# Loading the first pair's summed block beside the last convolution, in buffers of its own, in a hybrid Hyena and attention layer

## The chip, the cores and the metric

One core of a Trainium2 chip. The metric is the device time of one execution in microseconds (us). The kernel before was timed in three runs, and one execution was recorded by the hardware profiler. Five engines take part: TensorE (PE, with its weight loads PEld), VectorE (DVE), ScalarE (ACT), GpSimd (POOL) and SyncE (SP). [...]

## The reference

One layer works on 640 tokens (128 of a prompt, 512 latent tokens on a grid of 8 rows by 64 columns), 1024 channels and 16 heads of 64. All of it is float32.

```python
h = x * (1 + scale) + shift                      # scale, shift from the conditioning vector
z = h @ w_in                                     # 1024 x 10240: Hyena 3+1, q, k, v, gate, two mixing gates
v_h, x1, x0 = split(short_conv(hy))              # taps of three tokens
y_h = (fft_conv(v_h * x1, filter) + v_h * x1 * d) * x0
y_a = softmax(q k^T / 8 + bias, window + context) @ [v, ctx_v]   # prompt: all keys of the prompt
p_h = (y_h * silu(g_h)) @ w_bh
p_a = (y_a * silu(g_a)) @ w_ba
out = (sigmoid(m_h) * p_h + sigmoid(m_a) * p_a) @ w_out
x   = layer_norm(ALPHA * x + gate * out)
```

The outputs are the new x of both groups and the keys and values of the prompt.

## The kernel before

Float32 accuracy comes from three passes per product: each operand is split into a high part and a low part, and high x high, high x low and low x high are added up in PSUM. The 640 columns of tokens go through TensorE in two halves of 320. A weight tile of 1024 x 128 comes as `raw`; ACT copies its high part (`wh`), and the low part (`wl`) is made from the difference.

The first 360 us compute the modulation, the Hyena projections, the long convolution by quarters (its last part is `long_conv(3)` and `long_conv_back(3)`, with the stores of its gated result `yu` to `yu_d`), and values, queries, keys and two mixing gates of the first tiles. In this stretch a scheduler orders the instructions of each engine; `weave` lays `hand_over()` beside the last convolution. Instructions keep the order that the schedule gives them on each engine, and a DMA queue's engine stands still in front of an issue whose wait has not ended.

From about 360 us on the order is written out by hand (`manual_schedule`). First `first_gates()` makes two gate tiles (`gate_a`, the matmuls `mm` at L182) and the first weight blocks. Then follow 21 pairs. A pair is two tiles of `w_in`, multiplied with the tokens by a scheme of seven block products instead of eight (`pair_tile`): each product j of `ORDER = ("b11", "t2", "t3", "t1", "b21", "t4", "b22")` takes one weight block of 512 x 128 (here 128 x 512 on chip) and half of the columns, and is 12 matmuls of 320 columns. `t1` to `t4` are sums of token halves that were stored in `tok_d` before and come back by `load_sums` (names `t_00` to `t_11`: the first digit is the half of the rows, the second is high or low part). For a pair p the weight blocks are, in the order of products:

- `ra` left half, b11; loaded whole by `load_a` (512 KB);
- `s1`, the sum of s2 and a22, made by DVE in `sum1` (L1175), which after `sum6` (L1179) also serves as the last block;
- `s2` (in the trace `s<-wall`): a load of 256 KB, onto which POOL adds a second block of the weights with an accumulating DMA (L1167);
- `s3`: likewise, loaded by SP into half of `rb` and accumulated at L1168 (`rb_q` for the first pair);
- `ra` right half; `a22` (the other half of `rb`, or `rb_ql`).

For each block ACT makes the high part (`high`, L1185) and DVE the low part (`low`, L1193), `AHEAD = 4` blocks before TensorE uses it. TensorE's matmuls of the pairs are at L1232 (`sp` in PSUM; `t` or `hH`, `hL` the tokens). What a pair gives is used by `later` functions, run one or several half-blocks on (`tick`). `scratch()` copies second halves of the tokens inside `hH` and `hL`; it can start when the last matmul of the second gate tile has read them.

Between the half-blocks the loop calls `attend`: a visit is `tiled(i)` (scores of two blocks of a head at L947, PE; their reduction on DVE at L973, exponentials on ACT at L981, scaling on POOL at L1002 and L1004, and the products with the values of the blocks two visits before) or `turned(i)` (transposes of the probabilities at L1031, copied by ACT at L1026 as `pts`). Scores, transposes and products share the auxiliary PSUM banks. For the first head three visits are taken by a rule that begins after eight half-blocks; that gives half-blocks 9, 15 and 22 of 28.

In `hand_over` the mixing tiles `mx` (tanh at L870 on ACT) are stored to `mh_d` by SP's queue (L871). The first pair's blocks come from `first_blocks`: s2 takes a row of the pool `yhp` (tag "yh"), s3 and a22 the buffers "q" and "ql" of the slots of a later head.

## Time and profile before

| what | value |
|---|---|
| three runs | 904.39, 905.91, 906.86 us; median 905.91 |
| profiled execution | 904.75 us, its span 903.0 us |
| mean granted TensorE clock | 0.988 |
| PE busy | 872.3 us, 97% of the span, 6476 matmuls |
| DVE / ACT / POOL busy | 637.4 (71%) / 450.0 (50%) / 189.9 us (21%) |
| moved by DMA | 169.09 MB, mean 187 GB/s |

A row of the timeline gives the start, the duration, the engine, the line, the operation, out<-in, the shape and a count when rows are merged; in brackets stands how long the engine was idle before and what ended that. "x2" on a merged row means that its first instruction starts there and the duration covers both. For a DMA the duration on the issuing engine (SPq, POOLq) is the issue; the time to landing is listed on its own.

### The profile page before, as it was taken

How to read it: one execution, taken by the hardware profiler on the slowest of the kernel's cores; microseconds unless marked ns; L12 is line 12 of the kernel's file. 1: busy time of each engine (PE TensorE's matmuls, PEld its weight loads, DVE VectorE, ACT ScalarE, POOL GpSimd, SP SyncE). 2: the span in 40 equal slices, each digit the busy share in tenths (PEclk: the TensorE clock that was granted, in tenths of full speed). 3: DMA queues.
4: the chain of work that ended last, by engine and by line, in shares of the span. 5: the costliest groups of instructions: out<-in, count | busy, mean ns of one | idle time of the engine just before them, and what ended most of it. 6: DMA issues, size and time to landing. Idle time of an engine off the chain costs nothing. (4 is left out here: it accounts for less than half of the span.)

```text
span 903.0 us, 17145 instructions
## 1 busy us (share of the span) xinstructions
PE 872.3 (97%) x6476; PEld 841.3 (93%) x6476; DVE 637.4 (71%) x1215; ACT 450.0 (50%) x956; POOL 189.9 (21%) x216
## 2 busy tenths in 40 slices
PE   8999999999999999879999999999999999999995
PEld 7789999999899999779999999999999999999884
DVE  4896574984786557279777778777877677667566
ACT  4485545645554545156666665656566632233200
POOL 0020111210110110126354334433545200000000
PEclk9999999999999999889999999999999999999998
DMA  8976666876557685877686758576845586555332
GB/s 334 404 205 136 140 163 151 223 175 154 138 120 164 180 197 115 304 216 225 185 221 165 211 168 233 150 219 171 229 115 141 189 299 230 164 166 188 115 104 85
DMA packets 75247, 169.09 MB, mean 187 GB/s; under 512 B 11004, under 2 KB 28668, under 8 KB 75165
## 3 DMA queue, kind: packets, MB, share of 16 engines
q1 hardware_dynamic: 56492, 123.72, 41.5%
q0 software_dynamic: 13632, 39.33, 22.8%
q10 hardware_dynamic: 5040, 4.95, 1.6%
q8 instruction: 51, 0.84, 0.4%
q14 instruction: 32, 0.25, 0.1%
HBM read 143.32 MB, written 23.99 MB: 185 GB/s over the span
## 5 line engine op out<-in xcount | busy, mean ns | idle before, releaser
L1232 PE MATMUL sp<-t,wb 128*128 128x320 f32 x1008 | 161.1, 314 | 5.1 <-ACT wb L1185 5.1
L1232 PEld LDWEIGHTS sp<-t,wb 128*128 128x128 f32 x1008 | 152.3, 191 | 6.0 <-ACT wb L1185 5.4
L1232 PE MATMUL sp<-hH,wb 128*128 128x320 f32 x500 | 121.1, 313 | 0.0
L182 PE MATMUL mm<-hH,wh 128*128 128x320 f32 x336 | 84.1, 316 | 9.6 <-ACT mx L870 4.2
L1232 PEld LDWEIGHTS sp<-hH,wb 128*128 128x128 f32 x500 | 85.9, 188 | 2.8 <-issue 2.8
L182 PE MATMUL mm<-hL,wh 128*128 128x320 f32 x336 | 82.2, 313 | 0.4 <-DVE hL L329 0.4
L182 PE MATMUL mm<-hH,wl 128*128 128x320 f32 x336 | 81.5, 312 | 0.4 <-DVE wl L102 0.4
L1232 PE MATMUL sp<-hL,wb 128*128 128x320 f32 x250 | 77.3, 309 | 0.0
L162 POOL DMA_DIRECT2D wl<-wall x34 | 30.4, 893 | 220.7 <-ACT wl L161 201.8
L182 PEld LDWEIGHTS mm<-hH,wh 128*128 128x128 f32 x336 | 57.7, 190 | 12.0 <-ACT mx L870 4.4
L163 ACT ACTIVATE wh<-raw 128x1024 fp32r<-128x1024 f32 x34 | 36.2, 1064 | 63.0 <-PE mm L182 47.9
L1185 ACT ACTIVATE wb<-s 128x512 fp32r<-128x512 f32 x63 | 39.7, 631 | 42.8 <-PE sp L1232 19.4
L182 PEld LDWEIGHTS mm<-hL,wh 128*128 128x128 f32 x336 | 57.7, 190 | 1.5 <-DVE hL L329 1.2
L182 PEld LDWEIGHTS mm<-hH,wl 128*128 128x128 f32 x336 | 57.6, 190 | 1.3 <-DVE wl L102 0.9
L1193 DVE TENSOR_TENSOR wb<-s,wb 128x512 fp32r<-128x512 f32 x63 | 45.0, 716 | 18.8 <-ACT wb L1185 18.7
L1002 POOL TENSOR_SCALAR p<-p,sm 128x384 f32<-128x384 f32 x32 | 50.3, 1667 | 22.0 <-DVE sm L1000 15.8
L1002 POOL TENSOR_SCALAR edge<-edge,sm 128x320 f32<-128x320 f32 x32 | 41.7, 1405 | 52.1 <-DVE sm L1000 52.1
L1232 PEld LDWEIGHTS sp<-hL,wb 128*128 128x128 f32 x250 | 47.0, 188 | 0.0
L1509 PE MATMUL out<-woh,yhs 128*128 128x512 f32 (+1 forms) x176 | 45.7, 373 | 0.0
L1220 DVE TENSOR_TENSOR spare_hHp<-sp,yu 128x320 f32<-128x320 f32 x63 | 30.5, 483 | 16.8 <-PE sp L1232 11.5
L182 PE MATMUL mm<-yhs,wh 128*128 128x320 f32 x224 | 42.0, 309 | 0.0
L1509 PEld LDWEIGHTS out<-woh,yhs 128*128 128x128 f32 x176 | 32.0, 188 | 6.2
(415 smaller groups left out, 2251.7 us busy)
## 6 DMA issues: line engine op xcount, KB each, us to landing
raw<-wall SPq DMA_DIRECT2D x54, 512.0 KB, 3.9
wl<-wall POOLq DMA_DIRECT2D x34, 512.0 KB, 6.7
ra<-wall SPq DMA_DIRECT2D x21, 512.0 KB, 4.0
rb<-wall SPq DMA_DIRECT2D x40, 256.0 KB, 4.5
ada<-wada SPq DMA_DIRECT2D x16, 512.0 KB, 7.9
tm<-bias SPq DMA_DIRECT2D x16, 512.0 KB, 6.9
s<-wall SPq DMA_DIRECT2D x21, 256.0 KB, 4.7
s<-wall POOLq DMA_DIRECT2D x21, 256.0 KB, 4.6
```

What stands on the lines that cost most here:

```text
L162: nc.gpsimd.dma_start(wl, a["wall"][i], accum_op=ALU.add)
L163: nc.scalar.activation(wh, raw[:], AF.Copy)
L182: nc.tensor.matmul(ps[hf][:, :HALF], wt[k], x[:, hf * HALF : (hf + 1) * HALF], start=(i == 0 and k == 0), stop=(i == lead[2] and k == NK - ...
L1002: nc.gpsimd.tensor_scalar_mul(pv, pv, sm[:, 2, c : c + 1])
L1185: nc.scalar.activation(made[g][:, 0], sums_[g // 7][g % 7], AF.Copy)
L1193: nc.vector.tensor_tensor(made[g][:, 1], sums_[g // 7][g % 7], f(made[g][:, 0]), op=ALU.subtract)
L1220: nc.vector.tensor_tensor(c, dst, c if j == 3 else ps["u"], op=ALU.add)
L1232: nc.tensor.matmul(dst, wk, x(xi, k), start=j < 4 and k == 0 and i == 0, stop=k == 3 and i == 2, skip_group_check=True,)
L1509: ins = nc.tensor.matmul(dst, m[k][:, c0 : c0 + P], w[:, c : c + n], start=(first and k == 0), stop=(last and k == 5), skip_group_check=True,)
```

## The change

The change has five parts.

1. `first_blocks()` is called as soon as the slots exist, ahead of the values of the first head, instead of at the end of `hand_over`.
2. The sums get buffers of their own: `s2` one in `slots_q` for even pairs and one in `sp` for odd pairs, `s1` one in `sp`; before, they shared three buffers in `sp`. `ra` is taken up when it is needed (`block(g)`). In each pair the load of s2 now stands ahead of the two of rb. Of the buffers for the token sums, four are in `sp` and three in `tp` (before three and four).
3. The two stores of mixing tiles go out from ScalarE's queue.
4. The loads behind the hand-over are put in another order; those of t1, ra_1, t4 and the bias tiles (tm) follow `scratch()`.
5. The first head's three visits come after half-blocks 14, 20 and 27.

```diff
@@ hand_over
         out["slots_q"] = left.enter_context(tc.tile_pool(name="slots_q", bufs=1))
+        first_blocks()
         yield from chain(values(0), queries(0), keys(0))
...
         load_a(0)
-        first_blocks()
@@ mix_tile
-        nc.sync.dma_start(mh_d[n], th[:])
+        nc.scalar.dma_start(mh_d[n], th[:])
@@ attention_setup
-        homes[:] = [(sp, "tr", 3)] * 3 + [(tp, "tr", 4)] * 4 + [(yhp, "yh", NK + 1)]
+        homes[:] = [(sp, "tr", 4)] * 4 + [(tp, "tr", 3)] * 3 + [(yhp, "yh", NK + 1)]
@@ load_b, first_blocks, blocks
-        s2 = sp.tile([P, 512], F32, tag="s", bufs=3, name=f"s2_{p}")[:]
...
-        s2 = row(yhp, "yh", "s2_0")[:, :512]
...
+        s2 = (sp if p % 2 else out["slots_q"]).tile([P, 512], F32, tag="s", name=f"s2_{p}")[:]
+        load_to(s2, w0[:, :512])
         load_to(s3, w1[:, :512])
         load_to(a22, w1[:, 512:])
-        load_to(s2, w0[:, :512])
-        ra = raws.pop(("a", p))
-        sums_[p] = [ra[:, :512], None, s2, s3, ra[:, 512:], a22, None]
+        sums_[p] = [None, None, s2, s3, None, a22, None]
@@ sum1
-        s_[1] = s_[6] = sp.tile([P, 512], F32, tag="s", bufs=3, name=f"s1_{p}")[:]
+        s_[1] = s_[6] = sp.tile([P, 512], F32, tag="s1", name=f"s1_{p}")[:]
@@ after the hand-over
-    load_sums(1, SUMS[:2])
-    load_a(1)
+    load_sums(1, SUMS[:1])
     sums_of_second = load_b(1)
-    load_sums(1, SUMS[2:3])
-    biases[0] = [bias_tile(0)]
-    load_sums(0, SUMS[3:])
-    load_sums(1, SUMS[3:])
-    biases[0].append(bias_tile(1))
+    load_sums(1, SUMS[1:2])
...
         sums_of_second()
         scratch()
+        load_sums(1, SUMS[2:3])
+        load_a(1)
+        load_sums(0, SUMS[3:])
+        load_sums(1, SUMS[3:])
+        biases[0] = [bias_tile(h) for h in range(2)]
@@ the loop over heads
-                while taken * (n_main - late) < (done - late) * n_side:
+                while done in (14, 20, 27) if j == 0 else taken * n_main < done * n_side:
                     if next(side, StopIteration) is StopIteration:
                         break
                     taken += 1
+                    if j == 0:
+                        break
```

SP's queue around the hand-over, before. `t_10_4306` and `t_11_4308` are t2, 4310 and 4312 are t3, 4321 and 4323 are t1 (second half of the rows); `s_0` is the first pair's s2, `s_1` the second's. (In the changed kernel L1165, L1166 and L1234 are what L1167, L1168 and L1232 are before.)

```order
L63 DMA t_10_4306<-tok_d 128x640
L63 DMA t_11_4308<-tok_d 128x640
L871 DMA mh_d<-mx_4157 128x640
L63 DMA t_10_4310<-tok_d 128x640
L63 DMA t_11_4312<-tok_d 128x640
L63 DMA ra_4314<-wall 128x1024
L871 DMA mh_d<-mx_4218 128x640
L63 DMA rb_4316<-wall 128x512 x2
L63 DMA s_1_4317<-wall 128x512
L63 DMA s_0_4295<-wall 128x512
L63 DMA t_10_4321<-tok_d 128x640
L63 DMA t_11_4323<-tok_d 128x640
```

The same place after (t2, then s_1 and rb, t3 as 4315 and 4317, the scratch copies, t1 as 4450 and 4452):

```order
L63 DMA t_10_4306<-tok_d 128x640
L63 DMA t_11_4308<-tok_d 128x640
L63 DMA s_1_4311<-wall 128x512
L63 DMA rb_4310<-wall 128x512 x2
L63 DMA t_10_4315<-tok_d 128x640
L63 DMA t_11_4317<-tok_d 128x640
L63 DMA hH<-hHp 128x320 x2
L63 DMA hL<-hLp 128x320 x2
L63 DMA t_10_4450<-tok_d 128x640
L63 DMA t_11_4452<-tok_d 128x640
L63 DMA ra_4454<-wall 128x1024
```

The stores and the load of s_0 have left this stretch, and the loads of t1 and of `ra` stand behind the scratch copies.

POOL's queue, which issues the accumulating loads, from the last weight tiles of the scheduler's part on; before:

```order
L162 DMA wl_4054<-wall 128x1024
L1168 DMA rb_q<-wall 128x512
L162 DMA wl_4161<-wall 128x1024
L162 DMA wl_4222<-wall 128x1024
L162 DMA wl_4284<-wall 128x1024
L162 DMA wl_4289<-wall 128x1024
...
L1167 DMA s_1_4317<-wall 128x512
L1168 DMA rb_4316<-wall 128x512
L1167 DMA s_0_4295<-wall 128x512
```

and after:

```order
L162 DMA wl_4062<-wall 128x1024
L1165 DMA s_0_3755<-wall 128x512
L162 DMA wl_4169<-wall 128x1024
L1166 DMA rb_q<-wall 128x512
L162 DMA wl_4230<-wall 128x1024
L162 DMA wl_4292<-wall 128x1024
L162 DMA wl_4297<-wall 128x1024
...
L1165 DMA s_1_4311<-wall 128x512
L1166 DMA rb_4310<-wall 128x512
```

The accumulation onto s_0 moves from the end of the hand-over to the second row, and that of `rb_q` one place back.

TensorE's queue at the third visit, the transposes of the first head (`pt`), with what follows them; before:

```order
L1031 MATMUL pt_0_1_4801<-pack_380,p_0_1_4584 128x128 x3
L1031 MATMUL pt_1_1_4806<-pack_380,p_1_1_4585 128x128 x3
L1232 MATMUL sp_0_4674<-hH,wb_4687 128x320
L1232 MATMUL sp_0_4674<-hL,wb_4687 128x320
L1232 MATMUL sp_0_4674<-hH,wb_4687 128x320 x2
L1232 MATMUL sp_0_4674<-hL,wb_4687 128x320
L1232 MATMUL sp_0_4674<-hH,wb_4687 128x320 x2
```

and after, where the scores of the next head (`s_0_4891`) come two half-blocks later:

```order
L1031 MATMUL pt_1_1_4857<-pack_380,p_1_1_4646 128x128 x3
L1234 MATMUL sp_3_4752<-hH,wb_4724 128x320
L1234 MATMUL sp_3_4752<-hL,wb_4724 128x320
L1234 MATMUL sp_3_4752<-hH,wb_4724 128x320 x2
L1234 MATMUL sp_3_4752<-hL,wb_4724 128x320
L1234 MATMUL sp_3_4752<-hH,wb_4724 128x320
L1234 MATMUL sp_0_4876<-hH,wb_4764 128x320
L1234 MATMUL sp_0_4876<-hL,wb_4764 128x320
L1234 MATMUL sp_0_4876<-hH,wb_4764 128x320 x2
L1234 MATMUL sp_0_4876<-hL,wb_4764 128x320
L1234 MATMUL sp_0_4876<-hH,wb_4764 128x320
L947 MATMUL s_0_4891<-k_4565,q_4578 128x128
```

The transposes have moved to the end of the pair's visits, and only two half-blocks lie between them and the next scores; before, seven did.

More of the change, by code (lines that the diff above doesn't have):

```diff
@@ L1150, in load_b, with blocks @@
         rb = sp.tile([P, 1024], F32, tag="rb", bufs=2, name=f"rb{p}")
-        s2 = sp.tile([P, 512], F32, tag="s", bufs=3, name=f"s2_{p}")[:]
-        return blocks(p, s2, rb[:, :512], rb[:, 512:])
+        return blocks(p, rb[:, :512], rb[:, 512:])
     def first_blocks():
-        s2 = row(yhp, "yh", "s2_0")[:, :512]
-        blocks(0, s2, *(out["slots_q"].tile([P, NT], F32, tag=t, name=f"rb0_{t}")[:, :512] for t in ("q", "ql")))()
-    def blocks(p, s2, s3, a22):
+        blocks(0, *(out["slots_q"].tile([P, NT], F32, tag=t, name=f"rb0_{t}")[:, :512] for t in ("q", "ql")))()
+    def blocks(p, s3, a22):
         w0, w1 = (a["wall"][i] for i in pairs[p])
+        s2 = (sp if p % 2 else out["slots_q"]).tile([P, 512], F32, tag="s", name=f"s2_{p}")[:]
+        load_to(s2, w0[:, :512])
         load_to(s3, w1[:, :512])
         load_to(a22, w1[:, 512:])
-        load_to(s2, w0[:, :512])
-        ra = raws.pop(("a", p))
-        sums_[p] = [ra[:, :512], None, s2, s3, ra[:, 512:], a22, None]
+        sums_[p] = [None, None, s2, s3, None, a22, None]
         def summed():
@@ L1170, in blocks, with block @@
         return summed
+    def block(g):
+        p, j = divmod(g, 7)
+        return raws["a", p][:, 512 * (j // 4) : 512 * (j // 4) + 512] if j in (0, 4) else sums_[p][j]
     def sum1(p):
         s_ = sums_[p]
-        s_[1] = s_[6] = sp.tile([P, 512], F32, tag="s", bufs=3, name=f"s1_{p}")[:]
+        s_[1] = s_[6] = sp.tile([P, 512], F32, tag="s1", name=f"s1_{p}")[:]
         nc.vector.tensor_tensor(s_[1], s_[2], s_[5], op=ALU.add)
@@ L1178, in sum6 @@
         s_ = sums_[p]
-        nc.vector.tensor_tensor(s_[6], s_[4], s_[6], op=ALU.add)
+        nc.vector.tensor_tensor(s_[6], block(7 * p + 4), s_[6], op=ALU.add)
     def high(g):
@@ L1184, in high @@
             made[g] = wp.tile([P, 2, 512], F32R, tag=tag, bufs=2 if tag == "wh" else 3, name=f"wb{g}")
-            nc.scalar.activation(made[g][:, 0], sums_[g // 7][g % 7], AF.Copy)
+            nc.scalar.activation(made[g][:, 0], block(g), AF.Copy)
         elif (g - 7 * len(pairs)) % 2 == 0:
@@ L1192, in low @@
         if g < 7 * len(pairs):
-            nc.vector.tensor_tensor(made[g][:, 1], sums_[g // 7][g % 7], f(made[g][:, 0]), op=ALU.subtract)
+            nc.vector.tensor_tensor(made[g][:, 1], block(g), f(made[g][:, 0]), op=ALU.subtract)
         elif (g - 7 * len(pairs)) % 2:
@@ L1329, in yh_home @@
             return slot(0, ("q", "ql", "k", "kl")[i], f"yhs{i}", F32R)[:, :NT]
-        return row(yhp, "yh", f"yhs{i}", F32R)[:] if i < 13 else row(tp, "tr", f"yhs{i}", F32R, 4)[:]
+        return row(yhp, "yh", f"yhs{i}", F32R)[:] if i < 13 else row(tp, "tr", f"yhs{i}", F32R, 3)[:]
     yhH, yhL, yraw = [], [], {}
@@ L1374, in tile_hyena_natten_step @@
         scratch()
+        load_sums(1, SUMS[2:3])
[3 more added lines that the diff above has]
+        biases[0] = [bias_tile(h) for h in range(2)]
         for j in range(8):
-            late = 8 if j == 0 else 0
-            side, n_main, n_side = attend(j), N_PAIR * len(HEADS[j].split()), {0: 3, 7: N_ATT + 3}.get(j, N_ATT)
+            side, n_main, n_side = attend(j), N_PAIR * len(HEADS[j].split()), N_ATT if j < 7 else N_ATT + 3
             done = taken = 0
```

## The prediction

> **What bounds the kernel.** I read the page's head first, then the list of TensorE's waits, its timeline around the longest ones, and the window table for clock and transfers.

> ```profile
> span 903.0 us, 17145 instructions
> PE 872.3 (97%) x6476; PEld 841.3 (93%) x6476; DVE 637.4 (71%) x1215; ACT 450.0 (50%) x956; POOL 189.9 (21%) x216
> ...
> PEclk9999999999999999889999999999999999999998
> ```

> TensorE (PE) is busy 97% of the span, so time can only come from its few idle stretches and from slices below full clock. The two 8s inside the clock row are slices 17 and 18 of 22.6 us each (361 to 406 us), the place of the change. The list of TensorE's waits begins with the same place:

> ```profile
> PE sp L1232 <- ACT wb L1185: 5.1, 1, 5.1
> PE mm L182 <- ACT mx L870: 4.2, 1, 4.2
> ```

> No other single wait exceeds 1.8 us. The timeline of TensorE shows both, and what the 36 matmuls of three weight blocks take behind the second and at full clock:

> ```profile
> 365.53 0.96 PE L182 MATMUL mm<-hH,wh 128*128 128x320 f32 x2 [4.19 <-ACT mx L870]
> ...
> 381.62 0.31 PE L1232 MATMUL sp<-hH,wb 128*128 128x320 f32 x1
> ...
> 388.67 7.88 PE L1232 MATMUL sp<-t,wb 128*128 128x320 f32 x36 [5.13 <-ACT wb L1185]
> 396.38 0.31 PE L1232 MATMUL sp<-hH,wb 128*128 128x320 f32 x1
> ...
> 406.47 5.46 PE L1232 MATMUL sp<-t,wb 128*128 128x320 f32 x36
> ```

> Windows (the columns are PE, weight load, DVE, ACT, POOL busy with counts, granted clock, DMA share, GB/s):

> ```profile
> 365.50:370.00 4.50, 4.47 (x17) 4.43 (x18) 0.00 (x0) 1.07 (x3) 0.78 (x5) 0.53 0.95 302
> 370.00:381.60 11.60, 11.60 (x81) 11.60 (x80) 1.54 (x3) 1.28 (x3) 2.70 (x3) 1.00 1.03 376
> 383.40:388.60 5.20, 0.14 (x1) 0.00 (x0) 0.69 (x1) 0.61 (x2) 0.00 (x0) 0.82 0.79 196
> 388.60:396.40 7.80, 7.73 (x37) 7.51 (x38) 7.08 (x13) 4.33 (x10) 0.00 (x0) 0.68 0.67 214
> ```

> Each gap costs twice: the idle time, then about half clock (0.53, 0.68) until the clock is granted again. The second gap's cause, followed back through DVE, ACT, POOL and SP's queue:

> ```profile
> 387.26 0.69 DVE L1175 TENSOR_TENSOR s<-s,rb_ql 128x512 f32<-128x512 f32 x1 [10.56 <-DMA s<-wall]
> 387.99 1.15 ACT L1185 ACTIVATE wb<-s 128x512 fp32r<-128x512 f32 x2 [12.01 <-DVE s L1175]
> 376.53 0.90 POOL L1167 DMA_DIRECT2D s<-wall  x1 [10.25 <-DMA s<-wall]
> 365.83 0.32 SPq L871 DMA_DIRECT2D mh_d<-mx  x1
> 370.38 1.20 SPq L63 DMA_DIRECT2D s<-wall  x2
> ```

> SP loads s_0 as the second of the two rows at 370.38. POOL's accumulate onto it is the third of its run that starts at 376.53, and only when that lands can DVE make the sum (387.26), and ACT the weight block that TensorE waits for. The gap is a late load, not work.

> **The change, part by part.** *Early s_0.* After the change s_0's load stands directly ahead of rb_q's, and its accumulate one place ahead of rb_q's old one:

> ```profile
> 318.56 0.33 SPq L63 DMA_DIRECT2D rb_q<-wall  x1
> ...
> 325.79 0.90 POOL L1168 DMA_DIRECT2D rb_q<-wall  x1 [8.77 <-DMA raw<-wall]
> ```

> So s_0 is complete near 331 us, 45 us before use. What then sets the sum is the order on DVE and ACT, where it follows the first block:

> ```profile
> 374.69 0.77 ACT L499 ACTIVATE sg<-mm 128x320 f32<-128x320 f32 x2 [7.09 <-PE mm L182]
> 376.01 0.69 DVE L1193 TENSOR_TENSOR wb<-ra,wb 128x512 fp32r<-128x512 f32 x1
> ```

> Sum at 376.7, two blocks' high and low parts (0.6 to 0.7 each) done by 379.3; TensorE asks for them at 383.4. The margin is 4.1 us, so the wait of 5.13 goes: −5.13. Without it the clock has been at 1.00 since 370 and nothing lowers it, so the three blocks take 5.46, not 7.88: −2.42. [...] The rows have the loss itself, 2.42, and I go by them. The early stretch pays one more issue of 0.33 on SP and 0.9 on POOL, both waiting there anyway (8.77 idle): 0.

> *Stores of the mixing tiles on ScalarE's queue.* Two issues of about 0.33 under ACT's idle 7.09: 0. What is behind them on ACT is the second tanh, whose wait is this:

> ```profile
> 366.84 0.77 ACT L870 ACTIVATE mx<-mm 128x320 f32<-128x320 f32 x2 [1.04 <-DMA yu_d<-yu]
> yu_d<-yu POOLq DMA_DIRECT2D x4, 320.0 KB, 3.5
> ```

> It waits for one of POOL's stores; with SP's loads no longer held behind the tiles, more transfers compete with that. The tanh frees PSUM for the second gate tile, which TensorE does not begin before 373 (the first one's matmuls end near ACT's row at 374.69), so the store may land 6 us later than it did, beside a median of 3.5: 0. The first gap's wait (4.19) stays: its end is DVE's yu and ACT's tanh, and none of the change is ahead of them.

> *Loads after the hand-over.* s_1, rb_1 and t3 go out by about 369; then SP waits for the last reader of the scratch copies (hH, hL), and t1, ra_1, four t4 and the bias tiles tm follow:

> ```profile
> 376.30 1.60 SPq L63 DMA_DIRECT2D hH<-hHp  x2
> hH<-hHp SPq DMA_DIRECT2D x2, 160.0 KB, 10.8
> t<-tok_d SPq DMA_DIRECT2D x16, 320.0 KB, 6.0
> DMA to landing us min/median/max: 3.2/6.0/10.1
> tm<-bias SPq DMA_DIRECT2D x4, 512.0 KB, 5.3
> ```

> (The fourth row is for t in 300 to 400 us.) Now blocks follow each other every 1.76 us (381.62 to the end at 383.38), so t1's second half is asked for at 387.7 and t4's halves at 390.4 and 391.3. t1 is issued near 379.2 to 380.6: landing 385.6 with the median 6.0, and at worst 10.1 → 389.7, 2.0 late. In the built program each load on SP's queue also waits for the landing of the eighth load ahead of it: for t4_01, t4_10 and t4_11 those are scratch copies. These took 10.8 behind some 3 MB (two rb, two s, two t1, tm, three t4) that SP had issued just ahead. After the change what was issued earlier, some 3.2 MB from 359.6 on, is through by about 370 at 302 to 376 GB/s, so I take a copy at the quick end, 3.2 to 6: t4 issued by 383, there by 389. Cost 0; bounds 0 and 387.4 + 6.0 − 390.4 = 3.0. tm issued near 384 lands at 389 to 391, asked for at 395.5: 0.

> *Own buffers.* One s, one s1 and a lazily taken ra instead of shared tags; later pairs load s_2 first and then rb. TensorE's longest two waits both end before 389, and no wait of a weight block is listed after that, so later there is nothing to gain, and blocks made four ahead (7 us) cover a load shifted by one issue: 0.

> *Visits.* Scores of the first head move from half-block 9 to 14 (TensorE near 394), the next from 15 to 20, transposes from 22 to 27. Distances among these stay, but the next head's scores stand two half-blocks (1.8 us) behind the transposes, not seven. Rows of before:

> ```profile
> 397.36 0.33 PE L947 MATMUL s<-k,q 64*128 64x128 f32 x2
> 411.77 0.82 PE L1031 MATMUL pt<-pack,edge 128*128 128x128 f32 x6
> ...
> 412.29 0.87 ACT L1026 ACTIVATE pts<-pt 128x384 f32<-128x384 f32 x2 [0.94 <-PE pt L1031]
> 413.57 0.87 ACT L1026 ACTIVATE pts<-pt 128x384 f32<-128x384 f32 x2
> ...
> 408.20 1.18 POOL L1004 TENSOR_SCALAR pp<-pp,sm 128x128 f32<-128x128 f32 x2
> 403.00:411.70 8.70, 8.70 (x64) 8.32 (x63) 8.40 (x25) 7.10 (x22) 6.31 (x7) 1.00 0.47 100
> ```

> From the first scores to POOL's end is 12.0 us (397.36 to 409.38), to the transposes 14.4; 13 half-blocks keep that. The copies of the transposes end 2.7 us after these start (414.44 − 411.77), and the next scores, which take those PSUM banks, come after 3.1: margin 0.4. One weight copy of 0.64 ahead of them makes 0.2 late, two make 0.9. ACT was busy 7.10 of 8.70 there, so I take 0.5 between 0 and 0.9.

> Sum: 904.75 (the profiled execution, span 903.0 and 1.75 around it) − 5.13 − 2.42 + 0.5 = 897.7, a change of −7.05. The median of the three runs, 905.91, is 1.16 above the profiled one; from it the same change gives **898.9 us**. A measurement here tells about 0.3% (2.7 us) from no change.

> **Rivals.** *Late second-half loads* (t1 or t4 behind the scratch copies). For: the 10.8 us landing and the wait on the eighth load before; against: the queue ahead is empty by then. Price 2 to 3 us of idle, so 900.9 to 901.9. Whether that idle also lowers the clock no row decides: this one of 1.77 did not, while 4.19 and 5.13 did.

> ```profile
> 238.35 0.41 PE L182 MATMUL mm<-hH,wh 128*128 128x320 f32 x1 [1.77 <-ACT zs L484]
> 240.00:244.00 4.00, 4.00 (x29) 4.00 (x28) 4.00 (x10) 1.49 (x3) 0.56 (x1) 1.00 0.83 261
> ```

> If it does, 2.1 to 2.4 more: 904.3 at worst, inside "same". [...]

> *Moved visits stall TensorE like a gap*: the transposes or next scores wait 3.5 us or more (POOL's chain has 2.4 us to spare) and the clock falls: 898.9 + 3.5 + 2.4 = 904.8, no difference.

> *The change does not do it*: the sum still waits, for instance since DVE's queue holds it behind something of the hand-over: 905.9.

> *Slower*: visits now share pair 1 with the next head's. In 403 to 411.7 DVE is busy 8.40 of 8.70, and a visit's own DVE rows run from 398.43 to 401.2:

> ```profile
> 398.43 0.49 DVE L973 CUSTOM_DVE_ANT_0 edge<-s,tm 128x320 f32<-128x320 f32 x1 [1.35 <-PE s L947]
> ...
> 400.81 0.48 DVE L991 TENSOR_REDUCE sm<-s 128x1 f32<-128x128 f32 x2
> ```

> If those 2.8 us, with ACT's part (about 3) in turn, delay the weight blocks past their lead of 7 us (it decides once DVE's backlog exceeds that lead), TensorE waits in each of two pairs for 2.8 + 3: 11.6 − 0.5 more, 910. Against: backlog of about 3 us is less than half the lead.

> **Chances.** Forecast 0.67; late loads 0.17; stalling visits 0.06; no effect 0.05; slower 0.05. The forecast's own range is 897 to 900. For 8 in 10 the range needs the late loads as well, without most of the clock loss: 896.5 to 903.0, whose lower end is the full 7.55 with no stall (898.4) less the spread of the runs shown (1.5 below their median). Faster by over 0.3% (below 903.2): 0.67 + 0.16 = 0.83. Same: 0.01 of late loads, 0.06, 0.05: 0.12. Slower 0.05.

> **What the changed profile would show.** Right: no row of a weight block among TensorE's waits above 1 us, the 4.2 on the tanh still first; clock 1.00 from 370 to 400; three blocks in about 5.5 us from 383.4; DVE's sum near 377; POOL's accumulate onto s near 326; a span near 896. Wrong: a wait of t matmuls for a load (late loads), scores or transposes waiting for ACT or POOL above 1.5 us (visits), the sum still near 387 (no effect), or weight-block waits of 2 us and more after 400 (slower).

## The result and the profile after

The changed kernel takes 899.1 us (median of four runs, 897.27 to 900.61), the kernel before 905.97 (904.39 to 906.86). The ratio is 0.9925, with a 95% interval of 0.9902 to 0.9948: 4.7 to 8.9 us less. The forecast was 898.9, range 896.5 to 903.0. The profiled execution took 897.27 us, 7.48 less than the profiled one of before, at a mean clock of 0.993 instead of 0.988.

The head of the page, and the first three of TensorE's waits:

```profile
span 895.5 us, 17141 instructions
...
PEclk9999999999999999899999999999999999999998
```

```profile
PE mm L182 <- ACT mx L870: 4.2, 1, 4.2
PE mm L182 <- ACT hH L328: 2.9, 3, 1.3
PE mm L182 <- ACT zs L484: 2.4, 2, 1.8
```

One of the two 8s of the clock row is gone, and so is the wait of 5.1 us for a weight block; the wait for the tanh of the mixing tile is as long as it was. TensorE's timeline at the two places (L1177, L1187 and L1195 of the changed kernel are what L1175, L1185 and L1193 are before):

```profile
365.89 0.96 PE L182 MATMUL mm<-hH,wh 128*128 128x320 f32 x2 [4.22 <-ACT mx L870]
...
383.71 0.31 PE L1234 MATMUL sp<-hHp,wb 128*128 128x320 f32 x1
383.86 5.47 PE L1234 MATMUL sp<-t,wb 128*128 128x320 f32 x36
389.16 0.31 PE L1234 MATMUL sp<-hH,wb 128*128 128x320 f32 x1
```

The three blocks of t matmuls follow the first block without a gap and take 5.47 us instead of 7.88. The chain that had made them late, in the timelines of SP, POOL, DVE and ACT:

```profile
318.91 0.33 SPq L63 DMA_DIRECT2D s<-wall  x1
325.94 0.88 POOL L1165 DMA_DIRECT2D s<-wall  x1 [8.60 <-DMA new_v<-v]
377.03 0.69 DVE L1177 TENSOR_TENSOR s<-s,rb_ql 128x512 f32<-128x512 f32 x1
377.75 1.15 ACT L1187 ACTIVATE wb<-s 128x512 fp32r<-128x512 f32 x2 [1.36 <-DVE s L1177]
```

The load now goes out at 318.9 and the accumulate at 325.9; DVE makes the sum at 377.0 directly behind its preceding row, without waiting, and the first two weight blocks are ready four us ahead of use (VectorE's low parts of both end by 379.7, TensorE takes the first at 383.86). The loads that stood in doubt:

```profile
376.13 1.34 SPq L63 DMA_DIRECT2D hH<-hHp  x2
378.87 1.02 SPq L63 DMA_DIRECT2D t<-tok_d  x2
380.47 1.80 SPq L63 DMA_DIRECT2D t<-tok_d  x4
382.32 1.78 SPq L63 DMA_DIRECT2D tm<-bias  x2
DMA to landing us min/median/max: 2.0/2.1/2.1
```

(The last row is the landing of the two copies into hH, from SP's issues.) They took 2.1 us, not 10.8, so nothing behind them was held. The wait that did grow is the second tanh's, hidden as forecast:

```profile
369.81 0.77 ACT L870 ACTIVATE mx<-mm 128x320 f32<-128x320 f32 x2 [3.65 <-DMA yu_d<-yu]
```

It was 3.0 us later than before (366.84), and TensorE does not ask for its PSUM before 373.

### The profile page after: what moved, and what is told of

Read it like the earlier page. It is cut to its first block, busy times and chain, and to the rows that moved or that the text cites. A ratio compares the mean times of both kernels' runs of the same rounds, so it can differ in the third digit from the quotient of the medians.

```text
span 895.5 us, 17141 instructions
## 1 busy us (share of the span) xinstructions
PE 870.1 (97%) x6476; PEld 839.2 (94%) x6476; DVE 637.4 (71%) x1215; ACT 450.3 (50%) x956; POOL 190.2 (21%) x216
## 3 DMA queue, kind: packets, MB, share of 16 engines
q0 software_dynamic: 13632, 39.33, 22.6%
## 5 line engine op out<-in xcount | busy, mean ns | idle before, releaser
L1234 PE MATMUL sp<-t,wb 128*128 128x320 f32 x1008 | 158.9, 311 | 0.0
L1234 PEld LDWEIGHTS sp<-t,wb 128*128 128x128 f32 x1008 | 150.1, 188 | 0.5 <-issue 0.5
L1234 PE MATMUL sp<-hH,wb 128*128 128x320 f32 x500 | 121.0, 313 | 0.0
L182 PE MATMUL mm<-hH,wh 128*128 128x320 f32 x336 | 84.1, 316 | 9.6 <-ACT mx L870 4.2
L1234 PEld LDWEIGHTS sp<-hH,wb 128*128 128x128 f32 x500 | 86.1, 188 | 2.6 <-issue 2.6
L182 PE MATMUL mm<-hL,wh 128*128 128x320 f32 x336 | 82.2, 313 | 0.4 <-DVE hL L329 0.4
L182 PE MATMUL mm<-hH,wl 128*128 128x320 f32 x336 | 81.5, 312 | 0.4 <-DVE wl L102 0.4
L1234 PE MATMUL sp<-hL,wb 128*128 128x320 f32 x250 | 77.3, 309 | 0.0
L182 PEld LDWEIGHTS mm<-hH,wh 128*128 128x128 f32 x336 | 57.6, 190 | 12.0 <-ACT mx L870 4.5
L1195 DVE TENSOR_TENSOR wb<-s,wb 128x512 fp32r<-128x512 f32 x63 | 45.0, 716 | 20.3 <-ACT wb L1187 20.2
L182 PEld LDWEIGHTS mm<-hL,wh 128*128 128x128 f32 x336 | 57.7, 190 | 1.5 <-DVE hL L329 1.2
L182 PEld LDWEIGHTS mm<-hH,wl 128*128 128x128 f32 x336 | 57.6, 190 | 1.3 <-DVE wl L102 0.9
L1187 ACT ACTIVATE wb<-s 128x512 fp32r<-128x512 f32 x63 | 39.7, 631 | 32.0 <-PE sp L1234 20.3
L1234 PEld LDWEIGHTS sp<-hL,wb 128*128 128x128 f32 x250 | 47.0, 188 | 0.0
L182 PE MATMUL mm<-yhs,wh 128*128 128x320 f32 x224 | 42.0, 309 | 0.0
## 6 DMA issues: line engine op xcount, KB each, us to landing
raw<-wall SPq DMA_DIRECT2D x54, 512.0 KB, 3.8
wl<-wall POOLq DMA_DIRECT2D x34, 512.0 KB, 6.0
ra<-wall SPq DMA_DIRECT2D x21, 512.0 KB, 4.5
ada<-wada SPq DMA_DIRECT2D x16, 512.0 KB, 8.3
tm<-bias SPq DMA_DIRECT2D x16, 512.0 KB, 8.2
```

Source lines behind the costliest of these rows:

```text
L182: nc.tensor.matmul(ps[hf][:, :HALF], wt[k], x[:, hf * HALF : (hf + 1) * HALF], start=(i == 0 and k == 0), stop=(i == lead[2] and k == NK - ...
L1187: nc.scalar.activation(made[g][:, 0], block(g), AF.Copy)
L1195: nc.vector.tensor_tensor(made[g][:, 1], block(g), f(made[g][:, 0]), op=ALU.subtract)
L1234: nc.tensor.matmul(dst, wk, x(xi, k), start=j < 4 and k == 0 and i == 0, stop=k == 3 and i == 2, skip_group_check=True,)
```

## The experiments

**The early sum alone.** Parts 1 and 2 in the kernel before, with SP storing the mixing tiles, the old order of the loads and the old visits:

```diff
         out["slots_q"] = left.enter_context(tc.tile_pool(name="slots_q", bufs=1))
+        first_blocks()
...
+        s2 = (sp if p % 2 else out["slots_q"]).tile([P, 512], F32, tag="s", name=f"s2_{p}")[:]
...
+        s_[1] = s_[6] = sp.tile([P, 512], F32, tag="s1", name=f"s1_{p}")[:]
```

> The kernel before with parts 1 and 2 alone (early call, own buffers for the sums, the s2 load ahead of rb); stores of the mixing tiles on SP, the old order of the loads behind the hand-over, and the visits at 9, 15, 22 stay. Theory: the late s_0 was all of the gain, so about 899 us (-7), no wait on a weight block at 383, 36 matmuls in about 5.5 us. Rival (loads, stores or visits carry part of it): 901 to 904, with a wait of the t matmuls for a load or of the weight blocks left.

Measured: 897.74 us, ratio 0.9911 (0.9895 to 0.9928), as good as the whole change. The profiled execution was the slowest of four (900.7 us; POOL's last weight tile ahead of the first edited load is issued at 318.99, in the changed kernel at 316.45, so 2.5 us were lost before). Some 1.7 of them went at 240 us, in a stretch that no part of the change touches: behind an idle of 1.76 us the clock stood at half for 3.4 us, where the same idle of 1.77 in the kernel before had left it at full.

```profile
239.66 0.64 PE L182 MATMUL mm<-hH,wh 128*128 128x320 f32 x1 [1.76 <-ACT zs L484]
239.70:243.00 3.30, 3.30 (x12) 3.30 (x13) 3.30 (x9) 3.08 (x5) 0.58 (x1) 0.50 0.98 200
```

(In a row of a window the third number from the right is the granted clock.) So the row to read is the length of the blocks:

```profile
386.36 5.47 PE L1234 MATMUL sp<-t,wb 128*128 128x320 f32 x36
```

There is no wait ahead of it. From it to the end of the span are 512.5 us (898.9 − 386.36), with the whole change 511.6, before 514.3 behind its gap. So the sums are the whole gain, within what this can tell.

**The visits back.** In the changed kernel:

```diff
-                while done in (14, 20, 27) if j == 0 else taken * n_main < done * n_side:
+                while done in (9, 15, 22) if j == 0 else taken * n_main < done * n_side:
```

> The changed kernel with the first head's visits back at half-blocks 9, 15 and 22. Theory (the visits are worth nothing, the wait was all): 899 to 900; the bias tile tm0, issued near 382.5, lands at 388 to 389 and the first scores stand near 390, so at most 1 us of wait on VectorE and none on TensorE. Rival (the move is what makes room for the late bias tiles): TensorE waits 1.5 us or more for PSUM banks or weight blocks between 390 and 400, 901 or more.

Measured: 897.21 us, ratio 0.9909 (0.9895 to 0.9924); from the t matmuls to the end 511.7 us (895.2 − 383.53), the same as the changed kernel. No wait of TensorE stands there:

```profile
383.53 5.47 PE L1234 MATMUL sp<-t,wb 128*128 128x320 f32 x36
```

The visits' place is worth nothing in this order.

**The visits alone**, the same numbers 14, 20 and 27 in the kernel before.

> The kernel before with only the visits moved to 14, 20 and 27. Theory: the wait of 5.1 us stays, time 905 to 907, no difference. Rival (visits add pressure on VectorE in the second pair): 908 or more, with waits on weight blocks after 405.

Measured: 905.56 us, ratio 1.000 (0.999 to 1.001). The gap is there, the clock falls in it, and the 36 matmuls lose 2.86 us (8.33 − 5.47):

```profile
PE sp L1232 <- ACT wb L1185: 4.7, 1, 4.7
389.60 8.33 PE L1232 MATMUL sp<-t,wb 128*128 128x320 f32 x36 [4.73 <-ACT wb L1185]
```

**The stores on SP again**, in the changed kernel:

```diff
-        nc.scalar.dma_start(mh_d[n], th[:])
+        nc.sync.dma_start(mh_d[n], th[:])
```

> The changed kernel with the two stores of the mixing tiles back on SP's queue. Theory: SP's loads behind them are asked for only from 384 on, so 899 (no difference to the changed kernel). Rival (the stores were what held s_0 and the sums): a wait of 2 us or more at 384 comes back and the time is 902 or more.

Measured: 898.31 us, ratio 0.9923 (0.9908 to 0.9937): no difference to the changed kernel. SP stands in front of the two stores again, and t3 goes out at 370 instead of 362, still some 17 us ahead of use:

```profile
369.61 0.33 SPq L871 DMA_DIRECT2D mh_d<-mx  x1
369.99 0.96 SPq L63 DMA_DIRECT2D t<-tok_d  x2
385.14 5.47 PE L1234 MATMUL sp<-t,wb 128*128 128x320 f32 x36
```

**The wait put back alone.** In the changed kernel VectorE makes the first sum several times more, so the block is late with nothing else altered:

```diff
             if g == 1:
                 sum1(0)
+                for _ in range(17):
+                    nc.vector.tensor_tensor(sums_[0][1], sums_[0][2], sums_[0][5], op=ALU.add)
```

> The changed kernel with VectorE making the first pair's sum 18 times over (17 more): an idle of about 5.0 us at 384, all other parts of the change in place. Theory (the wait alone, with the clock it lowers, was the whole loss of the kernel before): 36 matmuls in 7.5 to 8.5 us, 906 to 907, about the time before. Rival (other parts of the change hold some of the gain): 902 to 904.

> The changed kernel with VectorE making the first pair's sum 14 times over (13 more of 0.61 us each, the same values), so only the wait comes back: the last sum starts near 385.0, TensorE begins the t matmuls near 386.4 instead of 383.9, an idle of 2.5 us, in length between the 1.77 that left the clock at full and the 4.19 that did not. Theory A (a short idle costs itself only): 36 matmuls in 5.5 us, 901.6 us. Theory B (any idle above about 2 us also lowers the clock): 7.5 to 8 us for the 36, 904.

> The changed kernel with 11 more sums instead of 13. By the two longer ones (3.85 with 13, 6.76 with 17, so 0.73 each) an idle of 2.4 us. [...] Theory B (2.4 us is enough): 7 us or more.

With 17 the time is 907.66 us, ratio to the kernel before 1.0012 (0.9999 to 1.0025): a loss as large as the whole gain is back, with nothing but VectorE's repeated sums added. This wait is longer than the old one, 6.76 us of idle instead of 5.13; with its 2.06 of clock (7.53 − 5.47) it makes 8.8, against 8.6 measured above the changed kernel. With 13 the time is 904.31 (0.997 to 0.9992 of the kernel before), 5.2 above the changed kernel, against 3.85 + 1.79 = 5.6 in its profile; with 11 it is 902.92, one run, 3.8 above. The idle was longer than I expected for 17 and 13, since a repeated sum takes 0.73 us and not 0.61. TensorE's timelines with 17, 13 and 11 (L1236, L1189 and L1197 are here what L1234, L1187 and L1195 are in the changed kernel):

```profile
392.17 7.53 PE L1236 MATMUL sp<-t,wb 128*128 128x320 f32 x36 [6.76 <-ACT wb L1189]
```

```profile
389.08 7.26 PE L1236 MATMUL sp<-t,wb 128*128 128x320 f32 x36 [3.85 <-ACT wb L1189]
```

```profile
387.84 0.56 PE L1236 MATMUL sp<-t,wb 128*128 128x320 f32 x2 [2.40 <-ACT wb L1189]
388.57 6.79 PE L1236 MATMUL sp<-t,wb 128*128 128x320 f32 x34 [0.17 <-DVE wb L1197]
```

Even an idle of 2.4 us cost clock: the 36 took 7.5 us (387.84 to the end of the second row) with 0.17 of waiting in it. Theory B held, in this one profile. Windows of that run:

```profile
385.40:387.80 2.40, 0.04 (x1) 0.00 (x0) 1.66 (x3) 0.64 (x2) 0.00 (x0) 1.00 0.92 310
387.80:389.40 1.60, 1.39 (x7) 1.13 (x8) 1.58 (x3) 1.60 (x5) 0.00 (x0) 1.00 1.03 404
389.70:392.70 3.00, 3.00 (x13) 3.00 (x12) 3.00 (x7) 1.77 (x4) 0.00 (x0) 0.50 0.75 297
393.10:396.10 3.00, 3.00 (x23) 3.00 (x22) 2.40 (x5) 1.29 (x3) 0.00 (x0) 1.00 0.88 333
```

The clock falls 1.7 us after TensorE is at work again, for about 3.4 us (at 0.4 us steps it is at half from 389.5 to 392.9). Before the change the same steps show half clock from 386.8 to 393.6, twice as long; from 388.67, where TensorE began, that is 4.9 us at half, a loss of 2.45, which is the 2.42 of the timeline.

**A better version: the other gap.** The 4.2 us left over are TensorE waiting for the first mixing tile's tanh, which waits for a row that VectorE's last yu still reads. In the changed kernel t1's first half takes that row instead, since its load has time:

```diff
-        load_sums(0, SUMS[:3])
+        load_sums(0, SUMS[:2])
...
     load_sums(1, SUMS[1:2])
+    load_sums(0, SUMS[2:3])
```

> The changed kernel with the loads of t1's first half moved from before the mixing tiles to behind t3's second half, so that the first mixing tile takes a row that has been free since 320 us and its tanh no longer waits for VectorE's last yu. Theory: the remaining wait of 4.2 us falls to about 0.5, the clock stays at full (another 2.1 us), t1 lands near 370 and is asked for near 381, so 893 us, 6 below the changed kernel. Rival (the next wait stands close behind: the second tanh, the scratch copies and the t loads now have 6 us less): TensorE waits 2 us or more between 372 and 390, 895 to 899.

Measured: 893.65 us, ratio to the kernel before 0.9864 (0.9844 to 0.9884), 5.5 below the changed kernel. The theory held, and two small waits are new:

```profile
362.75 0.74 PE L182 MATMUL mm<-hH,wh 128*128 128x320 f32 x2 [0.44 <-ACT mx L870]
378.88 5.46 PE L1234 MATMUL sp<-t,wb 128*128 128x320 f32 x36
```

```profile
PE s L947 <- ACT pts L1026: 1.0, 1, 1.0
PE sp L1234 <- DVE spare_hHp L1222: 0.7, 1, 0.7
```

The first is the wait that the prediction had feared for the moved visits: the next scores come two half-blocks behind the transposes. So the visits were varied in this kernel, to 9, 15, 22 and to 12, 18, 24 (the one line as above):

> e7 with the first head's visits at 9, 15 and 22. In e7 the visits cost two waits of TensorE, 0.7 and 1.0 us, at 404 and 409. Theory (the late place crowds them against the next head's): both go, 892. Rival (the move was made for the bias tiles): scores at 385 stand ahead of tm0's landing near 388, VectorE's queue stands for 2 to 3 us and the blocks behind it are late: a wait of 1 us or more between 386 and 395, 894 or more.

> e7 with the visits at 12, 18 and 24: the first scores at 388, just behind the bias tiles, the transposes five half-blocks ahead of the next scores. Theory: neither wait, 892 (1.7 below e7). Rival (the two small waits come from pair 1's own load on VectorE): they stay in other places, 893.5 to 894.

Measured: 892.48 us (ratio 0.9853, 0.9839 to 0.9868) and 892.3 us (0.9854, 0.9837 to 0.987). Neither has the two waits. With the early visits the rival's mechanism is there, but it stops at VectorE, since the weight blocks are four ahead:

```profile
387.97 0.49 DVE L973 CUSTOM_DVE_ANT_0 edge<-s,tm 128x320 f32<-128x320 f32 x1 [2.83 <-DMA tm<-bias]
```

At 892.3 us the last version is 13.7 us below the kernel before, 6.8 below the changed one.

## Why the prediction was right

- *The gap of 5.13 us goes*: shown. The wait is not in the list, the early sums alone give the whole gain, and a wait put back alone takes it away at its own price (8.6 us for 6.76 of idle, 5.2 for 3.85).
- *The clock comes with it, −2.42*: measured 7.88 − 5.47 = 2.41. The clock stood at half for 6.8 us there, from 386.8 to 393.6, and 4.9 us of them were work.
- *Stores on ScalarE's queue, order of the loads, own s1: 0*: shown for the stores, and for the loads and visits together by the early sums alone. The s1 of its own and the later pairs' s2 were in every run that had the gain, so that they are worth nothing is not shown. Parts 1 and 2 can't be parted by the call: with the buffer of its own and the call left at its old place the built program has the same order of rows on all five engines, so the scheduler loads early what has a free buffer. This was read from the order, not run. The profile before points the same way: there one call issued rb_q's load at 318.56 and s_0's at 370.38. In the built program of before, s_0's row is the one that the last yu had, so its load has to follow the store of that yu, which POOL issues at 365.30:

```profile
365.30 0.56 POOL L522 DMA_DIRECT2D yu_d<-yu  x1 [0.42 <-DVE yu L474]
```

- *Scratch copies 3.2 to 6 us*: 2.1. The step that a copy lands sooner with less issued ahead of it was right (10.8 us behind the ten loads that SP issued from 368.89 on, 2.1 us with none of SP's in the 12 us before), and its number cautious; the late-loads rival, which took the 10.8 us over, fell with it. t4's loads were issued by 382.3 at a largest landing of 7.1 us, so they were there by 389.4, and TensorE asks for t4 at 390.9.
- *Visits 0.5*: measured 0. ACT's four copies ran in one piece (410.82 to 412.44) and the scores came at 412.14 without a listed wait. The margin was truly small: with the blocks 5 us earlier it turned into 1.0 us.
- *Slower by DVE's backlog*: no weight block's wait is listed. The largest push on DVE in the runs, 2.83 us of standing still, did not reach TensorE either.
- Sum of the terms as measured: −5.13 − 2.41 + 0 = −7.54, against −7.48 between the two profiled executions and −6.87 between the medians. The 0.5 of the visits was the only term off. The interval of the ratio is 4 us wide, so hitting the median to 0.2 us is partly luck. The lower end of the range, 896.5, is 0.4 below its own working (898.4 − 1.5 = 896.9).
- One step was wrong without costing anything: the late-loads rival put 900.9 to 901.9 on an idle of 2 to 3 us, and the range took it without most of the clock loss. No run shows an idle of that length with the clock at full; by the run with 2.4 us idle it would have been about 3.8 us dearer than the forecast, 902.7. The row of 1.77 us, which the prediction took as an idle that leaves the clock at full, holds for that execution only: the early sums' profile has the same idle with the clock at half behind it.

## What to carry to other kernels

When TensorE's wait ends at a sum or a copy, follow it back to the load's issue and ask which buffer that load had to wait for; here a buffer of 2 KB per partition, free in time, was worth 7 us, and the three other parts of the same change nothing. Price a gap at its idle time and, for idles like these of 2.4 to 6.8 us, 1.8 to 2.9 us of clock beside it; a shorter one cost clock in one execution (1.76 us, with the early sums) and none in another (1.77 us, before). After a gap is closed, the next one of the same kind (a row still read by another engine) is worth looking for before anything is moved in the busy stretch.

## What the runs showed of the hardware

The clock's price did not grow with the gap: 1.9, 1.8, 2.9, 2.4 and 2.1 us for idles of 2.40, 3.85, 4.73, 5.13 and 6.76 us (the 36 matmuls less 5.47, and less the wait of 0.17 in the first; 4.73 is the visits alone, 5.13 the kernel before). What counts is how much of the half clock falls on work, of which it costs half: behind the gaps of 4.73, 5.13 and 6.76 us that was 5.9, 4.9 and 4.1 of 6.8 us, and with 2.40 us of idle all of the 3.4, which came only 1.7 us after the work had resumed.

```profile
362.90:369.70 6.80, 4.17 (x15) 4.13 (x16) 2.07 (x6) 1.53 (x4) 1.55 (x6) 0.50 0.61 195
369.80:386.70 16.90, 13.74 (x94) 13.48 (x92) 1.54 (x3) 1.28 (x3) 2.70 (x3) 1.00 1.05 338
386.80:393.50 6.70, 4.83 (x17) 4.61 (x18) 5.54 (x11) 4.31 (x9) 0.00 (x0) 0.50 0.43 138
```

The clock fell behind 1.76 us of idle with the early sums, and behind an idle of 1.30 us near 44 us in six of the twelve profiled executions (with the visits alone, it stood at half from 47.4 to 50.8). The length of the idle does not decide alone: in the kernel before both 1.77 us and the same 1.30 us left the clock at full. What decides it for such short idles these runs do not show. A short idle with 3.4 us of half clock on work behind it costs an estimated 1.7 us (half of the 3.4; 1.9 was measured behind 2.40 us), which is of the size of the spread between the runs of one kernel.
